# A decoder block on one core: the weights of group B's projections, of group A's queries and of the cross keys are split without GpSimd

## The chip, the core and the metric

The kernel runs on one core of a Trainium2 chip. A core has TensorE (matrix products and transposes), VectorE, ScalarE and GpSimd (elementwise work), SyncE (which here only issues transfers) and 16 DMA engines. The time is that of one execution on the device, in microseconds; the median of the runs shown is 813.85.

## The reference

The kernel computes one decoder layer for 512 tokens of width 1024 in float32, and a final RMSNorm:

```
h = rmsnorm(x);  proj = h @ w_in                       # one projection, 2984 columns
# group A (8 heads): indexer -> top-k keys per query -> attention over latents
index = sum_h relu(q_idx . k_idx) * w_idx;  sel = top_k(causal index, 128)
q_lat = q_nope @ w_uk;  s = q_lat . c_kv + q_rope . k_rope;  o_A = softmax(s[sel]) @ c_kv @ w_uv
# group B (8 heads): causal windows (128,1), (512,4), (2048,16), merged by softmax denominators
o_B = merge(dilated_attention(rope(q), rope(k), v))
x = x + concat(o_A, o_B) @ w_out
x = x + cross_attention(rmsnorm(x), rmsnorm(mem))      # 4 heads, 256 memory tokens
x = x + square(relu(rmsnorm(x) @ w_up)) @ w_down
out = rmsnorm(x)
```

## The kernel before

Every weight matrix is taken as the sum of a high and a low part, and a product as three TensorE products (`mm3`: high by high, high by low, low by high). So a weight passes four steps before TensorE can use it: SyncE's queue loads a piece of 128x1024 (or 128x768) into `wraw`; a cast makes the high part `whi` (line 130 on ScalarE, or line 128 on VectorE); a subtraction makes the low part `wlo` = `wraw` - `whi` (line 131, on GpSimd or VectorE); then TensorE reads both. `wraw` has three buffers, `whi` and `wlo` six each. `split_unit` does one piece; its letter says where: "v" casts on ScalarE and subtracts on VectorE, "p" casts on ScalarE and subtracts on GpSimd, "V" and "P" are the same with the cast on VectorE. `load_weight` splits a matrix into pieces and takes the letters in turn.

The stages, in the order in which they are written: norm and transposes of x; the indexer's projections and scores (lines 365 to 378: products and additions into `ghi` and `glo` on VectorE); group B's values, queries and keys (from line 381); for the four blocks of 128 queries, group B's attention (`attend`), interleaved with group A's queries (`queries_a`, two halves of four heads), the top-k rounds (`top_k`, lines 557 and 558: MAX8 and MATCH_REPLACE8 on VectorE, 16 rounds per block) and the norm of the memory tokens; group A's keys and attention; the cross keys (`keys_cross`, two halves of four pieces); output projection, cross-attention, MLP.

In `attend` a group of heads goes through a chain: scores on TensorE into one of two PSUM banks `sc`; line 426 on VectorE adds the bias and takes the extreme, which frees the bank; the exponential on ScalarE (line 428); reciprocal and scaling on VectorE (lines 429, 431); transposes on TensorE (`tp`, line 113), copies, and the product with the values (`pv`).

The order of the instructions on each engine is set by a scheduler when the program is built: it simulates a time line and places every instruction where its inputs and a free engine let it. So a change of an instruction's engine also changes the order of others. In the running program each engine takes its own list strictly in order.

Of the kernel before, what the change touches and what calls it, by code (L numbers as in the profile page):

```python
# [38 lines left out]
C_QN, C_QR, C_CKV, C_KR, C_QI, C_KI, C_WI, C_QB, C_KB, C_VB = (  # L39
    0, 512, 768, 896, 928, 1440, 1504, 1512, 2024, 2536)  # L40
# [24 lines left out]
def kernel(  # L65
# [16 lines left out]
    def nm(s):  # L82
        uid[0] += 1
        return f"{s}_{uid[0]}"

    def mtile(shape, dt, tag, bufs=1, pool=None):
        return (pool or main).tile(shape, dt, name=nm(tag), tag=tag, bufs=bufs)
# [7 lines left out]
    def bank_mm():  # L95
        return bank("mm", 3)

    def bank_tp():
        return bank("tp", 2)
# [12 lines left out]
    def tpose(*a, **k):  # L112
        ins = nc.tensor.transpose(*a, **k)  # L113
        if ordered[0]:
            tc.keep_in_program_order(ins)
# [8 lines left out]
    def split_unit(raw, hi, lo, how="v"):  # L124


        if how in "PV":
            nc.vector.tensor_copy(hi, raw)  # L128
        else:
            nc.scalar.copy(hi, raw)  # L130
        (nc.gpsimd if how in "pP" else nc.vector).tensor_tensor(lo, raw, f32(hi), op=ALU.subtract)  # L131

    def load_weight(w, segs, k0, how, between=None):


        n = sum(c1 - c0 for c0, c1 in segs)
        nk = 4 if n <= 256 else 2
        his, los = [], []
        for u in range(KD // nk):
            raw = mtile([P, nk, n], F32, "wraw", 3)  # L140
            hi = mtile([P, nk, n], F32R, "whi", 6)
            lo = mtile([P, nk, n], F32R, "wlo", 6)
            rows = w[(k0 + nk * u) * P:(k0 + nk * u + nk) * P, :].rearrange("(k p) c -> p k c", p=P)
            o = 0
            for c0, c1 in segs:
                nc.sync.dma_start(raw[:, :, o:o + c1 - c0], rows[:, :, c0:c1])
                o += c1 - c0
            split_unit(raw, hi, lo, how[u % 4])
            if between is not None:
                between(u)  # L150
            for j in range(nk):
                his.append(hi[:, j, :])
                los.append(lo[:, j, :])
        return his, los
# [17 lines left out]
    def mm3(dst, a, b, first=True, last=True, ks=None, again=False):  # L172


        n = len(a[0])
        for k in ks if ks is not None else range(n):
            mmul(dst, a[0][k], b[0][k], start=first and k == 0, stop=False, skip_group_check=again)
            mmul(dst, a[0][k], b[1][k], start=False, stop=False, skip_group_check=again)
            mmul(dst, a[1][k], b[0][k], start=False, stop=last and k == n - 1, skip_group_check=again)
# [36 lines left out]
    def split_from(ps, hi, lo):  # L216
        nc.scalar.copy(hi, ps)
        nc.vector.tensor_tensor(lo, ps, f32(hi), op=ALU.subtract)
# [23 lines left out]
    w_in0 = w_in[0]  # L242
# [27 lines left out]
    def h_tok(t):  # L270
        return ([hT[0][:, k, t * P:(t + 1) * P] for k in range(KD)],
                [hT[1][:, k, t * P:(t + 1) * P] for k in range(KD)])

    def rope(ps, heads, half, tabs, t, dst, dup=None):


        cos, sin, nsin = (tab[:, t, None, :].to_broadcast([P, heads, half]) for tab in tabs)
        r = r_mix[:, t:t + 1]
        n = heads * 2 * half
        rb = tmp.tile([P, 512], F32, name=nm("rb"), tag="rb", bufs=2)  # L280
        rbv = rb[:, :n].rearrange("p (h c f) -> p h c f", h=heads, c=2)
        if dup is None:
            ra = dst
        else:
            ra = tmp.tile([P, 512], F32, name=nm("ra"), tag="tok", bufs=2)[:, :n].rearrange(
                "p (h c f) -> p h c f", h=heads, c=2)

        def times(o, i, tab):
            nc.vector.scalar_tensor_tensor(o, i, r, tab, op0=ALU.mult, op1=ALU.mult)  # L289

        for c in range(2):
            times(ra[:, :, c, :], ps[:, :, c, :], cos)
        times(rbv[:, :, 0, :], ps[:, :, 1, :], nsin)
        times(rbv[:, :, 1, :], ps[:, :, 0, :], sin)
        if dup is None:
            nc.vector.tensor_tensor(*(a.rearrange("p h c f -> p h (c f)") for a in (dst, ra, rbv)), op=ALU.add)  # L296
        else:
            for c in range(dup):
                nc.vector.tensor_tensor(dst[:, :, c, :], ra.rearrange("p h c f -> p h (c f)"),
                                        rbv.rearrange("p h c f -> p h (c f)"), op=ALU.add)  # L300
# [78 lines left out]


    vB = [mtile([P, 2, 512], F32, f"u3{c}") for c in "ab"]
    wv = load_weight(w_in0, [(C_VB, C_VB + 512)], 0, "vpvp")
    for t in range(NT):
        ps = bank_mm()
        mm3(ps, h_tok(t), wv)
# [1 line left out]
    qkB = []  # L387
    for tag, col in (("u2a", C_QB), ("u2b", C_KB)):
        dst = mtile([P, 4, S], F32, tag)
        wt = load_weight(w_in0, [(col, col + 512)], 0, "pppp")  # L390
        for t in range(NT):
            ps = bank_mm()
            mm3(ps, h_tok(t), wt)
            tok = tmp.tile([P, 512], F32, name=nm("tok"), tag="tok", bufs=2)
            rope(ps.rearrange("p (h c f) -> p h c f", h=NH, c=2), NH, 32, tab64, t,
                 tok.rearrange("p (h c f) -> p h c f", h=NH, c=2))
            tp = bank_tp().rearrange("p (j t) -> p j t", j=4)
            for j in range(4):
                tpose(tp[:, j, :], tok[:, j * P:(j + 1) * P], ident)
            nc.scalar.copy(dst[:, :, t * P:(t + 1) * P], tp)  # L400
        qkB.append(dst)
# [70 lines left out]

    qA = mtile([96, NH, S], F32, "u1")
    def queries_a(g):
        wt = load_weight(w_in0, [(C_QN + 256 * g, C_QN + 256 * g + 256), (C_QR + 128 * g, C_QR + 128 * g + 128)], 0, "pppp")
        for t in range(NT):
            ps = bank_mm()
            mm3(ps[:, :384], h_tok(t), wt)
            tok = tmp.tile([P, 512], F32, name=nm("tok"), tag="tok", bufs=2)
            tokv = tok[:, :384].rearrange("p (h f) -> p h f", h=4)  # L480
            nc.scalar.activation(tokv[:, :, 0:64], ps[:, 0:256].rearrange("p (h f) -> p h f", h=4), AF.Copy,
                                 scale=r_mix[:, t:t + 1])
            rope(ps[:, 256:384].rearrange("p (h c f) -> p h c f", h=4, c=2), 4, 16, tab32, t,
                 tokv[:, :, 64:96].rearrange("p h (c f) -> p h c f", c=2))
            tp = bank_tp().rearrange("p (j t) -> p j t", j=4)
            for j in range(4):
                tpose(tp[0:96, j, :], tokv[:, j, :], ident)
            nc.scalar.copy(qA[:, 4 * g:4 * g + 4, t * P:(t + 1) * P], tp[0:96])
# [79 lines left out]
    def keys_cross(i):  # L568
        memT = state["memT"]
        if i == 0:  # L570
            state["kc"] = [mtile([P, KD, MEM], F32R, f"u2{c}") for c in "ab"]
        kc = state["kc"]
        wt = load_weight(w_kv[0], [(512 * i, 512 * i + 512)], 0, "pppp")
        for m in range(4):
            ps = bank_mm()
            msl = slice(m * P, (m + 1) * P)
            mm3(ps[:, :MEM], ([a[:, msl] for a in wt[0]], [a[:, msl] for a in wt[1]]),
                ([memT[:, 0, k, :] for k in range(KD)], [memT[:, 1, k, :] for k in range(KD)]))
            split_from(ps[:, :MEM], kc[0][:, 4 * i + m, :], kc[1][:, 4 * i + m, :])


    group_b(0)
    queries_a(0)
    top_k(1)
    group_b(1)
    top_k(2)
    queries_a(1)
    memory()
    group_b(2)
# [5 lines left out]
    for i in range(2):  # L595
        keys_cross(i)
# [109 lines left out]
    for i in range(2):  # L706
        wt = load_weight(w_q[0], [(512 * i, 512 * i + 512)], 0, "PPPP")
# [58 lines left out]
    for i in range(2):  # L766
        wt = load_weight(w_kv[0], [(D + 512 * i, D + 512 * i + 512)], 0, "ppPP")
# [75 lines left out]
    for g in range(4):  # L843
# [6 lines left out]
        for i in range(2):  # L850
            c0 = 1024 * g + 512 * i
            wt = load_weight(w_up[0], [(c0, c0 + 512)], 0, "vvvv")
# [143 lines left out]
```

## Time and profile before

| what | value |
|---|---|
| median of 3 runs | 813.85 us (813.5 to 816.56) |
| profiled execution | 814.07 us, its span 812.3 us |
| TensorE busy | 785.9 us (97%) |
| VectorE busy | 560.0 us (69%) |
| ScalarE busy | 382.5 us (47%) |
| GpSimd busy | 215.4 us (27%) |
| subtractions of line 131 on `wraw`, GpSimd | 59, together 139.3 us |
| the same on VectorE | 64, together 80.6 us |

A profile shows one execution. An engine's busy time is the sum of its instructions, and the span runs from the first to the last. A timeline row gives an instruction's start, its length, engine, line, what it writes and reads with the shape, how many alike follow at once, and in brackets how long the engine stood idle before it and what it waited for. The windows give each engine's busy time in a stretch, then TensorE's mean granted clock as a share of full speed.

### The profile page before, as it was taken

The numbers are of one execution on the slowest core, as the hardware profiler recorded it, in microseconds if no ns is written. First come the engines' busy times: TensorE is split into PE (matmuls) and PEld (weight loads), VectorE is DVE, ScalarE is ACT, GpSimd is POOL, SyncE is SP. The second block draws the span as 40 slices with busy tenths as digits, with TensorE's granted clock in tenths as the row PEclk, the third lists the DMA queues.
The fourth block names the chain that finished last, engine by engine and source line by source line (L and its number), as shares of the span: only waits on it lengthen the run. The fifth ranks groups of instructions, "written<-read, shape, count | busy, mean of one in ns | idle before, by whom it ended". The sixth has DMA issues, their size and how long they took to land.

```text
span 812.3 us, 11144 instructions
## 1 busy us (share of the span) xinstructions
PE 785.9 (97%) x4066; PEld 649.0 (80%) x4066; DVE 560.0 (69%) x1169; ACT 382.5 (47%) x743; POOL 215.4 (27%) x164
## 2 busy tenths in 40 slices
PE   6799999999999999999999999999999999999995
PEld 5688878985698778788898888888888888888884
DVE  6775999998668844634683447767776776676674
ACT  5444333457955634222472545533552455345544
POOL 4733143130613406544510201110111011201132
PEclk9899999999999999999999999999999999999998
DMA  8441232202423303322540333496439743963482
GB/s 288 133 119 38 69 105 73 66 1 78 156 79 105 105 1 103 102 80 79 181 140 18 103 104 82 101 229 212 99 83 209 225 100 85 223 221 85 89 164 103
DMA packets 53223, 94.12 MB, mean 116 GB/s; under 512 B 5265, under 2 KB 11057, under 8 KB 53169
## 3 DMA queue, kind: packets, MB, share of 16 engines
q1 hardware_dynamic: 44464, 76.64, 30.1%
q0 software_dynamic: 8704, 16.78, 12.4%
q8 instruction: 32, 0.52, 0.3%
q14 instruction: 23, 0.18, 0.1%
HBM read 90.78 MB, written 2.10 MB: 114 GB/s over the span
## 4 chain that ended last, share of the span: by engine, by line
PE 82%; DVE 10%; issue 3%; POOL 2%; ACT 2%; DMA 1%; SPq 0%; POOLq 0%; ACTq 0%; DVEq 0%
PE mm L107 61%; PE sc L107 11%; PE tp L113 5%; PE pv L107 3%; PE tp L107 2%; DVE glo L558 1%; DVE m L557 1%; DVE ghi L377 1%; ACT whi L130 1%; DMA u2b<-in_w_down_dram 1%; DVE whi L128 1%; DVE rb L289 1%; DVE kk L296 0%; DMA u2a<-in_x_dram 0%; DVE wlo L131 0%
## 5 line engine op out<-in xcount | busy, mean ns | idle before, releaser
L131 POOL TENSOR_TENSOR wlo<-wraw,whi 128x1024 fp32r<-128x1024 f32 (+2 forms) x59 | 139.3, 2379 | 186.8 <-ACT whi L130 156.7
L107 PE MATMUL mm<-whi,h 128*128 128x512 f32 (+2 forms) x536 | 165.3, 377 | 6.9 <-DVE h L231 3.5
L130 ACT CAST whi<-wraw 128x1024 fp32r<-128x1024 f32 (+3 forms) x111 | 114.0, 1029 | 93.9 <-PE mm L107 42.4
L107 PE MATMUL mm<-h,whi 128*128 128x512 f32 (+1 forms) x448 | 153.2, 366 | 0.0
L107 PE MATMUL mm<-u,whi 128*128 128x512 f32 x320 | 125.0, 390 | 0.0
L107 PE MATMUL mm<-u,wlo 128*128 128x512 f32 x320 | 124.7, 390 | 0.0
L107 PEld LDWEIGHTS mm<-whi,h 128*128 128x128 f32 x536 | 100.6, 194 | 21.6 <-DVE h L231 3.9
L107 PE MATMUL mm<-wlo,h 128*128 128x512 f32 (+2 forms) x280 | 104.9, 376 | 0.1
L131 DVE TENSOR_TENSOR wlo<-wraw,whi 128x1024 fp32r<-128x1024 f32 (+1 forms) x64 | 80.6, 1260 | 29.7 <-ACT whi L130 29.4
L107 PEld LDWEIGHTS mm<-h,whi 128*128 128x128 f32 x448 | 80.7, 188 | 14.7 <-issue 1.2
L895 POOL DMA_DIRECT2D u2b<-in_w_down_dram x24 | 32.6, 1369 | 224.5 <-DMA wraw<-in_w_down_dram 120.6
L107 PE MATMUL mm<-whi,ghi 128*128 128x512 f32 x192 | 76.2, 397 | 0.0
L107 PE MATMUL mm<-wlo,ghi 128*128 128x512 f32 x192 | 75.7, 394 | 0.0
L107 PE MATMUL mm<-whi,glo 128*128 128x512 f32 x192 | 75.1, 391 | 0.0
L107 PEld LDWEIGHTS mm<-u,wlo 128*128 128x128 f32 x320 | 60.1, 188 | 12.5
L107 PEld LDWEIGHTS mm<-u,whi 128*128 128x128 f32 x320 | 60.1, 188 | 12.2
L131 DVE TENSOR_TENSOR wlo<-u2b,whi 128x1024 fp32r<-128x1024 f32 x32 | 39.1, 1225 | 30.2 <-ACT whi L130 30.2
L107 PEld LDWEIGHTS mm<-wlo,h 128*128 128x128 f32 x280 | 54.1, 194 | 7.2 <-DVE wlo L131 0.5
L130 ACT CAST whi<-u2b 128x1024 fp32r<-128x1024 f32 x32 | 33.6, 1052 | 48.0 <-DMA u2b<-in_w_down_dram 39.5
L428 ACT ACTIVATE p<-p,mx 128x128 f32<-128x128 f32 (+3 forms) x64 | 35.9, 563 | 26.4 <-DVE mx L426 26.3
L862 ACT ACTIVATE sq<-r 128x512 f32<-128x512 f32 x32 | 20.2, 631 | 49.1 <-DVE r L860 49.1
L860 DVE SCALAR_TENSOR_TENSOR r<-mm,rT 128x512 f32<-128x512 f32 x32 | 22.0, 688 | 30.3 <-PE mm L107 23.2
(250 smaller groups left out, 1433.7 us busy)
## 6 DMA issues: line engine op xcount, KB each, us to landing
wraw<-in_w_up_dram SPq DMA_DIRECT2D x32, 512.0 KB, 4.7
wraw<-in_w_down_dram SPq DMA_DIRECT2D x24, 512.0 KB, 6.1
u2b<-in_w_down_dram POOLq DMA_DIRECT2D x24, 512.0 KB, 7.6
wraw<-in_w_in_dram SPq DMA_DIRECT2D x16, 512.0 KB, 4.0
wraw<-in_w_kv_cross_dram SPq DMA_DIRECT2D x16, 512.0 KB, 3.7
wraw<-in_w_out_dram SPq DMA_DIRECT2D x8, 512.0 KB, 3.8
wraw<-in_w_q_cross_dram SPq DMA_DIRECT2D x8, 512.0 KB, 3.7
wraw<-in_w_o_cross_dram SPq DMA_DIRECT2D x8, 512.0 KB, 3.7
```

The costliest lines, as they stand in the source:

```text
L107: ins = nc.tensor.matmul(*a, **k)
L113: ins = nc.tensor.transpose(*a, **k)
L128: nc.vector.tensor_copy(hi, raw)
L130: nc.scalar.copy(hi, raw)
L131: (nc.gpsimd if how in "pP" else nc.vector).tensor_tensor(lo, raw, f32(hi), op=ALU.subtract)
L289: nc.vector.scalar_tensor_tensor(o, i, r, tab, op0=ALU.mult, op1=ALU.mult)
L377: nc.vector.scalar_tensor_tensor(acc[b], rl[:, :n], wh, acc[b], op0=ALU.mult, op1=ALU.add)
L428: nc.scalar.activation(pr[:, c], pr[:, c], AF.Exp, bias=mx[:, i:i + 1], scale=-1.0, accum_out=sm[:, i:i + 1])
L557: nc.vector.max(m8, acc[b])
L860: nc.vector.scalar_tensor_tensor(r, ps, 0.0, rows_ready[0], op0=ALU.max, op1=ALU.mult)
L862: nc.scalar.activation(sq, r, AF.Square)
L895: nc.gpsimd.dma_start(xw[:, u], src, accum_op=ALU.add)
```

## The change

Four calls of `load_weight` get other letters, so that 26 subtractions run on VectorE instead of GpSimd: 2 of group B's values (line 382), 8 of its queries and keys (line 390), 8 of 128x768 of group A's queries (line 475) and 8 of the cross keys (line 573). The casts stay on ScalarE, and other weights keep their letters.

```diff
     vB = [mtile([P, 2, 512], F32, f"u3{c}") for c in "ab"]
-    wv = load_weight(w_in0, [(C_VB, C_VB + 512)], 0, "vpvp")
+    wv = load_weight(w_in0, [(C_VB, C_VB + 512)], 0, "vvvv")
...
         dst = mtile([P, 4, S], F32, tag)
-        wt = load_weight(w_in0, [(col, col + 512)], 0, "pppp")
+        wt = load_weight(w_in0, [(col, col + 512)], 0, "vvvv")
...
     def queries_a(g):
-        wt = load_weight(w_in0, [(C_QN + 256 * g, C_QN + 256 * g + 256), (C_QR + 128 * g, C_QR + 128 * g + 128)], 0, "pppp")
+        wt = load_weight(w_in0, [(C_QN + 256 * g, C_QN + 256 * g + 256), (C_QR + 128 * g, C_QR + 128 * g + 128)], 0, "vvvv")
...
         kc = state["kc"]
-        wt = load_weight(w_kv[0], [(512 * i, 512 * i + 512)], 0, "pppp")
+        wt = load_weight(w_kv[0], [(512 * i, 512 * i + 512)], 0, "vvvv")
```

The first place is VectorE at the end of the indexer's block 1 (`glo_110`) and the start of block 2 (`ghi_109`). Before, from the product that ends at 72.48:

```order
L377 SCALAR_TENSOR_TENSOR glo_110_645<-rl_685,weff,glo_110_645 128x256
L377 SCALAR_TENSOR_TENSOR glo_110_645<-rl_691,weff,glo_110_645 128x256
L378 TENSOR_TENSOR glo_110_645<-glo_110_645,bias 128x128
L557 MAX m_297_1555<-glo_110_645 128x8
L558 MATCH_REPLACE glo_110_645<-m_297_1555,glo_110_645 128x256
L375 TENSOR_SCALAR ghi_109_644<-rl_698,weff 128x384
```

The same place after the change; wlo_938 and wlo_944 are pieces of group B's queries, wlo_1103 and wlo_1109 of its keys:

```order
L377 SCALAR_TENSOR_TENSOR glo_110_645<-rl_685,weff,glo_110_645 128x256
L131 TENSOR_TENSOR wlo_938<-wraw_936,whi_937 128x1024
L377 SCALAR_TENSOR_TENSOR glo_110_645<-rl_691,weff,glo_110_645 128x256
L131 TENSOR_TENSOR wlo_944<-wraw_942,whi_943 128x1024
L378 TENSOR_TENSOR glo_110_645<-glo_110_645,bias 128x128
L131 TENSOR_TENSOR wlo_1103<-wraw_1101,whi_1102 128x1024
L557 MAX m_297_1555<-glo_110_645 128x8
L375 TENSOR_SCALAR ghi_109_644<-rl_698,weff 128x384
L558 MATCH_REPLACE glo_110_645<-m_297_1555,glo_110_645 128x256
L131 TENSOR_TENSOR wlo_1109<-wraw_1107,whi_1108 128x1024
```

Four subtractions now stand between the indexer's instructions, which wait behind them and behind their casts.

The second place is VectorE in group B's attention of the last block (p_2303 to p_2362 are its softmax tiles, in the order of the heads). Before:

```order
L431 TENSOR_SCALAR p_2303<-p_2303,rc_2306 128x512
L429 RECIPROCAL rc_2323<-sm_2322 128x1
L431 TENSOR_SCALAR p_2320<-p_2320,rc_2323 128x512
L426 ISA p_2345,mx_2346<-sc_2343,bias 128x512
L426 ISA mx_2346 128x1
L429 RECIPROCAL rc_2348<-sm_2347 128x1
L431 TENSOR_SCALAR p_2345<-p_2345,rc_2348 128x512
```

After; wlo_3047 and wlo_3053 are pieces of the cross keys, wlo_2194 (a few rows ahead) the split of group A's key weights, sel_2298 the end of the last top-k:

```order
L558 MATCH_REPLACE ghi_109_644<-m_493_2295,ghi_109_644 128x512
L426 ISA p_2362,mx_2363<-sc_2360,bias 128x512
L426 ISA mx_2363 128x1
L131 TENSOR_TENSOR wlo_3047<-wraw_3045,whi_3046 128x1024
L429 RECIPROCAL rc_2323<-sm_2322 128x1
L218 TENSOR_TENSOR glo_266_1364<-pv_2021,ghi_265_1363 128x2x128
L560 TENSOR_SCALAR sel_2298<-ghi_109_644 128x512
L429 RECIPROCAL rc_2348<-sm_2347 128x1
L131 TENSOR_TENSOR wlo_3053<-wraw_3051,whi_3052 128x1024
L431 TENSOR_SCALAR p_2320<-p_2320,rc_2323 128x512
L429 RECIPROCAL rc_2365<-sm_2364 128x1
L431 TENSOR_SCALAR p_2345<-p_2345,rc_2348 128x512
```

Two subtractions of the cross keys, the last top-k round and another head's score step have come between the softmax steps of p_2320 and p_2345.

The third place is TensorE at the same heads (mm_2203 to mm_2230 are group A's keys). Before:

```order
L107 MATMUL mm_2215<-cT_238,wlo_2194 128x512
L113 MATMUL tp_2328<-ident,p_2320 128x128 x4
L107 MATMUL sc_2402<-u2b_1100,u2a_923 128x512
L113 MATMUL tp_2353<-ident,p_2345 128x128 x4
L107 MATMUL sc_2427<-u2b_1100,u2a_923 128x512
L107 MATMUL sc_2444<-u2b_1100,u2a_923 128x512
L107 MATMUL mm_2221<-cT_238,whi_2193 128x512
```

After:

```order
L107 MATMUL mm_2215<-cT_238,wlo_2194 128x512
L107 MATMUL sc_2402<-u2b_1100,u2a_923 128x512
L113 MATMUL tp_2328<-ident,p_2320 128x128 x4
L113 MATMUL tp_2353<-ident,p_2345 128x128 x4
L107 MATMUL mm_2221<-cT_238,whi_2193 128x512
L107 MATMUL mm_2221<-cT_239,whi_2193 128x512
L107 MATMUL mm_2221<-cT_238,wlo_2194 128x512
```

The scores of sc_2402 have moved ahead of the transposes of p_2320, and those of sc_2427 to a place behind nine products of group A's keys, the transposes of p_2362 and a product with the values.

## Rows read from the trace of the kernel before

**Rows 1.** Busy time of each engine; the chain that ended last, by engine

```profile
PE 785.9 (97%) x4066; PEld 649.0 (80%) x4066; DVE 560.0 (69%) x1169; ACT 382.5 (47%) x743; POOL 215.4 (27%) x164
...
PE 82%; DVE 10%; issue 3%; POOL 2%; ACT 2%; DMA 1%; SPq 0%; POOLq 0%; ACTq 0%; DVEq 0%
```

**Rows 2.** Windows: columns in the first row, one stretch in each other

```profile
core 0: us, PE busy (x) PEld busy (x) DVE busy (x) ACT busy (x) POOL busy (x), PEclk, DMA share, GB/s
44.00:72.48 28.48, 28.48 (x139) 23.46 (x139) 16.34 (x32) 12.74 (x25) 7.57 (x3) 1.00 0.27 74
...
182.00:204.60 22.60, 21.46 (x137) 12.24 (x135) 17.85 (x68) 17.32 (x53) 0.00 (x0) 1.00 0.29 81
72.48:204.60 132.12, 129.48 (x731) 104.22 (x730) 123.21 (x369) 65.54 (x154) 38.11 (x20) 1.00 0.23 66
204.60:222.00 17.40, 16.52 (x93) 11.40 (x93) 12.00 (x27) 16.16 (x31) 12.64 (x6) 0.90 0.52 167
222.00:295.00 73.00, 72.14 (x567) 58.85 (x565) 52.77 (x160) 38.35 (x103) 21.41 (x9) 1.00 0.25 80
```

**Rows 3.** Timeline of VectorE, 70 to 82 (start, length, ...)

```profile
71.99 0.48 DVE L377 SCALAR_TENSOR_TENSOR glo<-rl,weff,glo 128x256 f32<-128x256 f32 x1 [1.36 <-ACT rl L372]
75.01 2.44 DVE L377 SCALAR_TENSOR_TENSOR glo<-rl,weff,glo 128x256 f32<-128x256 f32 x1 [2.53 <-ACT rl L372]
77.48 2.38 DVE L378 TENSOR_TENSOR glo<-glo,bias 128x128 f32<-128x128 f32 x1
...
80.76 1.58 DVE L375 TENSOR_SCALAR ghi<-rl,weff 128x384 f32<-128x384 f32 x1
```

**Rows 4.** Timeline of VectorE, 100 to 111

```profile
100.68 0.27 DVE L378 TENSOR_TENSOR ghi<-ghi,bias 128x128 f32<-128x128 f32 x1
...
101.73 1.93 DVE L375 TENSOR_SCALAR ghi<-rl,weff 128x512 f32<-128x512 f32 x1
...
106.87 1.93 DVE L377 SCALAR_TENSOR_TENSOR ghi<-rl,weff,ghi 128x512 f32<-128x512 f32 x1
...
110.44 0.73 DVE L377 SCALAR_TENSOR_TENSOR ghi<-rl,weff,ghi 128x512 f32<-128x512 f32 x1
```

**Rows 5.** Timeline of GpSimd, the four subtractions at 74.77

```profile
74.77 9.83 POOL L131 TENSOR_TENSOR wlo<-wraw,whi 128x1024 fp32r<-128x1024 f32 x4 [16.41 <-ACT whi L130]
```

**Rows 6.** Timeline of VectorE, a subtraction at 34.47 and its successor

```profile
34.47 1.22 DVE L131 TENSOR_TENSOR wlo<-wraw,whi 128x1024 fp32r<-128x1024 f32 x1
35.60 0.35 DVE L296 TENSOR_TENSOR kk<-kk,rb 128x64 f32<-128x64 f32 x2
```

**Rows 7.** Timeline of VectorE, 204 to 212

```profile
204.11 0.49 DVE L431 TENSOR_SCALAR p<-p,rc 128x512 f32<-128x512 f32 x1
204.51 0.68 DVE L218 TENSOR_TENSOR wlo<-tp,whi 128x512 fp32r<-128x512 f32 x1
205.11 0.68 DVE L426 CUSTOM_DVE_ANT_0 p<-sc,bias 128x512 f32<-128x512 f32 x1
...
206.55 0.42 DVE L218 TENSOR_TENSOR glo<-pv,ghi 128x256 fp32r<-128x256 f32 x1 [0.75 <-ACT ghi L217]
...
208.89 1.49 DVE L431 TENSOR_SCALAR p<-p,rc 128x512 f32<-128x512 f32 x1
...
211.02 1.30 DVE L544 COPY h<-mm 64x512 f32<-64x512 f32 x2
```

**Rows 8.** Timeline of TensorE, 115.34 and 206 to 212

```profile
115.34 0.63 PE L113 MATMUL tp<-ident,tok 128*128 128x128 f32 x4 [0.95 <-DVE tok L296]
...
206.87 0.60 PE L113 MATMUL tp<-ident,p 128*128 128x128 f32 x4
207.40 1.12 PE L107 MATMUL sc<-u2b,u2a 64*128 64x512 f32 x2
...
211.04 1.23 PE L107 MATMUL sc<-u2b,u2a 64*128 64x512 f32 x2 [0.88 <-DVE mx L426]
```

**Rows 9.** Timeline of ScalarE, a cast at 80.86

```profile
80.86 1.05 ACT L130 CAST whi<-wraw 128x1024 fp32r<-128x1024 f32 x1 [0.54 <-DMA wraw<-in_w_in_dram]
```

## The prediction

> **What bounds the kernel now.** I read the page first: TensorE is busy for 785.9 of 812.3 us, VectorE for 560.0, and the chain that ended last is TensorE for 82% and VectorE for 10% [rows 1]. The reader is to see an engine that hardly ever rests, so an edit on other engines changes the time only through the moments in which TensorE waits for them, or newly has to.
>
> Next I read the busy time by stretch [rows 2], because an average over the span hides where VectorE is full. Between 72.48 and 204.60 us, where the indexer, the top-k rounds and group B's attention lie, TensorE is busy for 129.48 of 132.12 us and VectorE for 123.21. Its 8.91 us of rest are mostly at the end: 4.75 in 182 to 204.6, so 4.16 before that. Before this stretch (44 to 72.48) VectorE rests 12.1 of 28.5 us, after it (222 to 295) 20.2 of 73. Thus work added to VectorE is free on either side and not in the middle.
>
> Third, I read VectorE's instructions in order of time. A product-and-add of line 377 takes 0.48 us, but 2.44 at 75.01; the mask addition of line 378 takes 0.27 at its normal size, but 2.38 at 77.48 [rows 3, 4]. Both lie inside GpSimd's four subtractions that run from 74.77 for 9.83 us [rows 5]. A VectorE instruction with two operands in the on-chip memory, or a 128x384 scaling, is held until GpSimd's subtraction ends. So GpSimd's help is not free: it costs VectorE some us.
>
> Last, TensorE's own waits in the middle are few: 0.95 us at 115.34 for a rotated query tile, 0.88 at 211.04 for a score bank, and a stretch at 204.6 to 222 with a mean granted clock of 0.90, part of it at the lower of the two levels, 1.2 instead of 2.4 GHz, after the rest at 211.04 [rows 2, 8].
>
> **The change part by part.** It moves 26 subtractions (line 131) from GpSimd to VectorE: 2 for group B's values, 8 for its queries and keys, 8 of 128x768 for group A's queries, 8 for the cross keys. The casts stay on ScalarE, the loads on SP's queue in the same order; GpSimd's list of instructions loses 26 rows.
>
> *Price of one.* A subtraction of 128x1024 on VectorE lasts 1.22 us, and the next instruction starts 1.13 us after it [rows 6]; I use 1.13. For 128x768 there is no row. It lies between the spacing of a 128x512 subtraction (line 218 at 204.51, the next start at 205.11: 0.60) and 1.13 [rows 6, 7]; I take the middle, 0.87. On GpSimd one took about 2.4 us (9.83 / 4) [rows 5], off everyone's path but for the blocking.
>
> *First four* (both of the values, two of the queries; 4 x 1.13 = 4.5 us). They fall before 72.48, in 12.1 us of rest: nothing.
>
> *The middle.* From the seventh line-377 product (ends 72.48) to the scaling of p_2345 (starts 204.11, ends 204.60) VectorE now also has nine subtractions of 128x1024 (two of the queries, four of the keys, three of the cross keys, which the new order puts ahead of group B's last softmaxes): 9 x 1.13 = 10.2. Eight of 128x768 for group A's queries: 8 x 0.87 = 7.0 (4.8 to 9.0 by the bounds). Some rows that stood behind p_2345 now stand ahead of it: a line-218 subtraction of 128x512 (0.68), a score step (0.68) and a line-218 subtraction of 128x256 (0.42), less the overlap of about 0.1 each, with a reciprocal of 0.16: 1.7 [rows 7]. Sum 18.9.
>
> *What goes.* Blocked instructions return to their normal size: 2.44 - 0.48 = 1.96, 2.38 - 0.27 = 2.11, the 128x384 scaling 1.58 - 0.49 = 1.09 (0.49 is the 128x512 one, so at least this), and the 128x512 ones at 106.87 and 101.73, 1.93 - 0.73 = 1.20 and 1.93 - 0.49 = 1.44 [rows 3, 4, 7]. Sum 7.8 in the middle. The blocked scaling at 208.89 (1.49 for 0.49) lies behind p_2345 and gives 1.0 back there, which is within what I take for hand-offs below.
>
> *VectorE's new time.* Busy 123.2 + 18.9 - 7.8 = 134.3. I keep the 4.16 of rest before 182, which is made of waits for casts and scores; the 4.75 behind it is filled, since the new order pulls top-k rounds of the last block apart into it. p_2345 is then scaled at 72.48 + 134.3 + 4.2 = 211.0, 6.4 later than at 204.60; p_2320, one reciprocal and one scaling before it, at about 210.3.
>
> *What TensorE feels.* It transposes p_2320 at 206.87 [rows 8], so it waits 210.3 - 206.9 = 3.4. In the new order the scores of sc_2402 (1.12) go ahead of this transpose: -1.1. The scores of sc_2427 wait for a bank that VectorE clears three copies of line 544 (about 0.65 each), a scaling (0.49), wlo_3059 (1.13), a 128x256 subtraction (0.42) and a score step (0.68) later [rows 7], 4.6 us behind 211.0, so at about 215.6; TensorE has some 4.5 us of other work behind 210.3 (an estimate from the spacing of its rows, [rows 8]) and is there at 214.8: +0.8. The wait of 0.88 at 211.04 has another neighbour and goes: -0.9. Small hand-offs, and a clock that falls after a rest as it does in 204.6 to 222 (17.4 x 0.10 = 1.7 us there [rows 2]), lie between 0 and 4; I take 1.7, the one such row. Sum 3.4 - 1.1 + 0.8 - 0.9 + 1.7 = +3.9.
>
> *The last four* (cross keys, 4 x 1.13 = 4.5; the fifth is wlo_3059 above). They lie in 204.6 to 222 with 5.4 us of rest and 222 to 295 with 20.2 [rows 2]: nothing, and TensorE reads their results microseconds after. If that cover is gone, each costs at most its 1.1.
>
> *The added wait.* A VectorE subtraction waits for its cast, and the cast for its load; at 80.86 ScalarE's cast had to wait 0.54 for the load [rows 9]. VectorE works in order, so what is behind such a subtraction (softmax steps, line 377) waits as well. In the new order wlo_3053 stands directly ahead of p_2320's scaling. Lower bound 0, upper some 4 us (a subtraction's whole 2.4 on GpSimd and the load's wait); I take 0 for the forecast and keep the rest for a rival.
>
> The profiled execution took 814.07 us for a span of 812.3, and the median of the runs is 813.85. So 814.07 + 3.9 = 818.0, or **817.8** on the median's scale.
>
> *A rule weighed.* The blocked rows [rows 3 to 5] say that GpSimd's help costs VectorE 7.8 us here. The Trainium skill, page "SBUF — State Buffer", section "SBUF: two separate sides", says that VectorE and GpSimd share one port pair as an exclusive lock, and that the loser blocks for the whole instruction; the trace agrees (2.44 for 0.48). By that alone VectorE would be early by 7.8 and the kernel faster, which is rival A. Against it stands the page "Perfetto Trace Analysis", section "Optimizing Scalar/DVE Operations": a saturated VectorE may hand work even to GpSimd, though with the shared port this may not help. The rows decide between the two: 17.2 us of subtractions come in, 7.8 go out.
>
> **Rivals.** *A, the locks decide.* VectorE's added work is in the top-k filler, which nobody awaits, and what TensorE awaits comes earlier, since nothing is held any more. Then the waits of 0.95 and 0.88 go, and the slow stretch of 1.7: 813.85 - 3.5 = 810.3, and some tenths of smaller waits less, about **810**. For it: the blocked instructions are real, and the new order was free to place the subtractions. Against it: VectorE's sum is positive by 9.4 without the pulled rows, and only 4.75 us of rest are there to take it.
>
> *B, slower than forecast.* The mechanism is VectorE's order: a subtraction whose cast is late holds the softmax steps behind it between 184 and 222, once ahead of p_2320 and once at the bank of sc_2427. Two waits of some 2 us (a load's wait of 0.54 and a cast of 1.05 each [rows 9], and a hand-off) come on top: 817.8 + 4 = **822**. It decides from the point where a cross-key cast ends later than VectorE reaches its subtraction. For it: ScalarE is busy 16.16 of 17.4 us in 204.6 to 222. Against it: VectorE itself is late there, so that casts have more time.
>
> *C, no change.* The forecast's lateness is 3.4 us at one place. If the 128x768 price is at its lower end (7.0 to 4.8: -2.2) and the rows pulled ahead of p_2345 come at moments of rest after all (-1.7), the 3.4 are gone, and what is left of the sum (0.8 - 0.9 and some hand-offs) makes 813.85 + 1 = **815**.
>
> **How the numbers follow.** A change of 0.5% is 4.1 us, about what a measurement here can tell: faster is below 809.8, slower above 817.9. Chances: forecast 0.40 with 815 to 821 as its own range, A 0.14, C 0.25, B 0.21. Slower is B and half of the forecast, 0.41; faster is most of A with its tail below 809.8, 0.13; the rest 0.46. The range goes from A's edge, 810, to 824, beyond B, and leaves out about 2 in 10.
>
> **What would show it.** In the profile after, VectorE should be busy for about 9 us more between 72 and 205, line 377's instructions should all be near 0.5 to 0.7, and GpSimd empty there but for the norm of the memory. The step on lateness is right if TensorE waits 2 to 5 us around 207 to 216 for VectorE's scalings or score steps; it is wrong if these waits are under 1 us in all (C), or if the first transposes of group B's queries lose their waits and the stretch ends earlier (A). Waits of VectorE for ScalarE's casts ahead of softmax steps would show B. A load landing late, with SP's queue in another order, would make the whole sum wrong.

## The result, and the profile after

The changed kernel takes 1.0055 times the time of the kernel before, with a 95% interval of 1.0033 to 1.0077; on the median of the kernel before in the same comparison, 815.43 us (21 runs, 813.46 to 818.21), that is 819.9 us. Its own 21 runs have a median of 826.96 us and fall into two groups that the granted clock tells apart, 816.0 to 819.3 us (10 runs, median 816.8, mean clock 0.990 to 0.994) and 827.0 to 835.6 us (11 runs, 0.963 to 0.976); the ratio leaves out the 8 slowest runs of the second group, so half of the executions are slower than it says. The profile after shows a run of the second group (829.65 us, span 827.9); experiment 1 gave a profile of the first (816.43 us, span 814.7).

The page of the profile after, TensorE's line of busy times and the granted clock in 40 slices:

```profile
PE 799.6 (97%) x4066; PEld 655.3 (79%) x4066; DVE 572.1 (69%) x1195; ACT 383.4 (46%) x743; POOL 156.1 (19%) x138
...
PEclk9899999995799999999999999999999999999998
```

GpSimd's work fell from 215.4 to 156.1 us, and VectorE's rose from 560.0 to 572.1 [rows 1]. TensorE is busy for 13.7 us more with the same 4066 products. The clock is down to 5 and 7 tenths in slices 10 and 11 (186 to 228 us). The windows around them, in the profile after (columns as in [rows 2]):

```profile
core 0: us, PE busy (x) PEld busy (x) DVE busy (x) ACT busy (x) POOL busy (x), PEclk, DMA share, GB/s
180.00:187.00 7.00, 5.67 (x28) 3.18 (x26) 6.90 (x25) 5.39 (x16) 0.00 (x0) 0.91 0.62 159
187.00:215.00 28.00, 26.75 (x88) 13.73 (x88) 18.00 (x59) 11.10 (x32) 0.00 (x0) 0.50 0.05 17
215.00:222.00 7.00, 7.00 (x33) 3.88 (x32) 6.34 (x15) 6.51 (x13) 0.00 (x0) 0.90 0.45 153
```

The same windows in the profile without the fall:

```profile
180.00:187.00 7.00, 5.67 (x27) 2.73 (x25) 6.99 (x26) 5.50 (x17) 0.00 (x0) 1.00 0.72 188
187.00:215.00 28.00, 25.05 (x139) 13.99 (x140) 27.94 (x81) 22.53 (x53) 0.00 (x0) 1.00 0.27 85
215.00:222.00 7.00, 7.00 (x52) 4.63 (x52) 5.68 (x15) 5.30 (x11) 0.00 (x0) 1.00 0.53 152
```

In 180 to 187 both have TensorE busy for 5.67 of 7 us. Then the one runs 28 us at 0.50 (1.2 GHz), which is 14 us of work lost, and the other at 1.00. The first meets two more waits of 0.62 us in that stretch:

```profile
192.58 1.12 PE L107 MATMUL pv<-pT,u3a 128*64 128x128 f32 x8 [0.62 <-ACT pT L441]
...
202.19 1.12 PE L107 MATMUL pv<-pT,u3a 128*64 128x128 f32 x8 [0.62 <-ACT pT L441]
```

The spans differ by 827.9 - 814.7 = 13.2. So what the change does is read from the second profile, and what the fall costs from the difference.

VectorE in the second profile, the instructions that answer to [rows 3, 4] and one of the moved 128x768 subtractions:

```profile
75.46 0.48 DVE L377 SCALAR_TENSOR_TENSOR glo<-rl,weff,glo 128x256 f32<-128x256 f32 x1
...
77.08 0.28 DVE L378 TENSOR_TENSOR glo<-glo,bias 128x128 f32<-128x128 f32 x1
...
78.76 0.40 DVE L375 TENSOR_SCALAR ghi<-rl,weff 128x384 f32<-128x384 f32 x1
...
104.61 0.95 DVE L131 TENSOR_TENSOR wlo<-wraw,whi 128x768 fp32r<-128x768 f32 x1
```

None of these is blocked: 0.48 for 2.44, 0.28 for 2.38, 0.40 for 1.58. The smaller subtraction lasts 0.95, and the next instruction starts 0.87 behind it (at 105.48). VectorE's windows in the same profile:

```profile
72.43:182.00 109.57, 109.42 (x613) 93.77 (x611) 102.87 (x300) 49.32 (x107) 7.32 (x6) 1.00 0.23 64
182.00:204.60 22.60, 19.68 (x115) 10.45 (x116) 22.60 (x80) 16.31 (x44) 0.00 (x0) 1.00 0.26 70
73.86:210.88 137.02, 133.17 (x737) 105.47 (x737) 131.27 (x391) 71.02 (x163) 7.32 (x6) 1.00 0.26 73
```

Between 182 and 204.6 it has no rest at all (22.60 of 22.60; before, 17.85 [rows 2]). TensorE's listed waits from 182 us to 222, where the kernel before has 0.88 at 211.04 [rows 8] and three smaller ones (0.33, 0.49, 0.29; 1.99 in all):

```profile
182.35 0.41 PE L113 MATMUL mm<-ident,ghi 128*128 128x128 f32 x2 [0.50 <-DVE rb L289]
183.58 0.91 PE L107 MATMUL sc<-u2b,u2a 64*128 64x384 f32 x2 [0.82 <-DVE mx L426]
...
189.56 0.66 PE L107 MATMUL pv<-pT,u3a 128*64 128x128 f32 x8 [0.62 <-ACT pT L441]
...
195.22 0.66 PE L107 MATMUL pv<-pT,u3a 128*64 128x128 f32 x8 [0.62 <-ACT pT L441]
...
202.12 0.66 PE L113 MATMUL tp<-ident,wraw 128*128 128x128 f32 x4 [0.30 <-ACT pT L441]
...
210.57 1.08 PE L113 MATMUL tp<-ident,p 128*128 128x128 f32 x8 [0.78 <-DVE rc L429]
...
214.86 0.66 PE L107 MATMUL pv<-pT,u3a 128*64 128x128 f32 x8 [0.42 <-DVE glo L218]
```

They add up to 4.06 us, while from 72 to 182 TensorE now rests only 109.57 - 109.42 = 0.15 us (1.5 before [rows 2]).

TensorE's own work has changed as well. Score products of two heads that follow each other directly run side by side, so that four take the time of two; in the new order none of the 512-wide ones do. Two rows, the first from the kernel before, the second from the second profile:

```profile
197.76 1.13 PE L107 MATMUL sc<-u2b,u2a 64*128 64x512 f32 x4
...
196.51 1.12 PE L107 MATMUL sc<-u2b,u2a 64*128 64x512 f32 x2
```

Group B's scores of all four widths keep TensorE busy for 19.1 us in the kernel before and for 20.9 in the second profile. So between these two profiles TensorE rests 1.4 us less up to 182 and 2.1 more from there to 222, works 1.8 longer on scores, and is spared the 1.7 of the lower clock at 204.6 to 222: +0.8 together. The spans differ by 2.4 (814.7 and 812.3) and the medians by 1.3 (816.8 and 815.4); the remainder is not resolved.

### The profile page after: what moved, and what is told of

Read it like the earlier page. It is cut to its first block, busy times and chain, and to the rows that moved or that the text cites. A ratio compares the mean times of both kernels' runs of the same rounds, so it can differ in the third digit from the quotient of the medians.

```text
span 827.9 us, 11151 instructions
## 1 busy us (share of the span) xinstructions
PE 799.6 (97%) x4066; PEld 655.3 (79%) x4066; DVE 572.1 (69%) x1195; ACT 383.4 (46%) x743; POOL 156.1 (19%) x138
## 4 chain that ended last, share of the span: by engine, by line
PE 86%; DVE 6%; issue 3%; POOL 2%; ACT 2%; DMA 1%; POOLq 0%; ACTq 0%
PE mm L107 63%; PE sc L107 13%; PE tp L113 5%; PE pv L107 3%; PE tp L107 2%; DVE wlo L131 1%; DMA u2b<-in_w_down_dram 1%; ACT whi L130 1%; DVE whi L128 1%; DVE kk L296 0%; PE mm L113 0%; DVE glo L218 0%; DMA u2a<-in_x_dram 0%; DVE xr L920 0%; DVE nmx L734 0%
## 5 line engine op out<-in xcount | busy, mean ns | idle before, releaser
L131 DVE TENSOR_TENSOR wlo<-wraw,whi 128x1024 fp32r<-128x1024 f32 (+2 forms) x90 | 110.4, 1227 | 32.6 <-ACT whi L130 32.1
L131 POOL TENSOR_TENSOR wlo<-wraw,whi 128x1024 fp32r<-128x1024 f32 (+1 forms) x33 | 79.0, 2404 | 138.8 <-PE mm L107 77.5
L107 PEld LDWEIGHTS mm<-whi,glo 128*128 128x128 f32 x192 | 36.0, 188 | 8.3 <-issue 0.7
L107 PEld LDWEIGHTS mm<-whi,ghi 128*128 128x128 f32 x192 | 36.1, 188 | 7.4 <-issue 0.5
```

Source lines behind the costliest of these rows:

```text
L107: ins = nc.tensor.matmul(*a, **k)
```

## The experiments

Ratios are to the kernel before on the same chip, with 95% intervals. Theory 1 is the prediction's: VectorE's load pushes its work late, and TensorE waits for it; here it was joined by the clock that falls behind such waits.

**1. The changed kernel again** (no edit).

> The changed kernel once more, beside the parts below. Theory 1 (VectorE's load): up to 182 us TensorE is some 2 us ahead of the kernel before, since VectorE is no longer held; then the last block's top-k rounds, pushed late by the added subtractions, stand ahead of softmax steps, and TensorE waits twice at 183 to 185 (0.5 and 0.8 us in the trace after). Where the granted clock then falls to 0.5 for some 28 us the time is 827 to 830, where it does not, 816 to 819. Rival 2 (the clock falls by itself, whatever the kernel does): the same stretch falls in the parts as well, and in the kernel before. Rival 3 (late casts of the cross keys hold softmax steps): VectorE waits for ScalarE's casts between 196 and 222.

Ratio 1.0062 (1.0023 to 1.0100); 6 of 12 runs at 815.8 to 816.8 us, 6 at 826.8 to 833.6, near the two ranges that theory 1 gave. Of the 114 runs of the kernel before in all comparisons here none was over 822.04, so a fall of this length belongs to the changed kernel: against rival 2. What VectorE does at the two waits:

```profile
182.38 0.68 DVE L557 MAX8 m<-ghi 128x8 f32<-128x512 f32 x1
182.98 0.54 DVE L426 CUSTOM_DVE_ANT_0 p<-sc,bias 128x384 f32<-128x384 f32 x1
...
208.82 1.21 DVE L131 TENSOR_TENSOR wlo<-wraw,whi 128x1024 fp32r<-128x1024 f32 x1
209.94 0.48 DVE L431 TENSOR_SCALAR p<-p,rc 128x512 f32<-128x512 f32 x1
...
210.41 0.47 DVE L431 TENSOR_SCALAR p<-p,rc 128x512 f32<-128x512 f32 x1
```

At 182.38 a top-k MAX8 stands between the rotation and the score step of 182.98, and TensorE, which needs the bank, waits till 183.58. At 208.82 wlo_3053 stands ahead of p_2320's scaling, and p_2345 is scaled at 210.41. None of these rows has an idle time for a cast, and between 184 and 222 only one subtraction waited for one (0.73, at 221.5, behind the softmax steps in question): against rival 3.

**2. Group B's projections alone.**

```diff
-    wv = load_weight(w_in0, [(C_VB, C_VB + 512)], 0, "vpvp")
+    wv = load_weight(w_in0, [(C_VB, C_VB + 512)], 0, "vvvv")
-        wt = load_weight(w_in0, [(col, col + 512)], 0, "pppp")
+        wt = load_weight(w_in0, [(col, col + 512)], 0, "vvvv")
```

> Only group B's projections are split without GpSimd (10 subtractions). Theory 1: the instructions blocked at 75 to 112 return to normal (7.8 us of VectorE back for 6.8 us of subtractions in the middle), TensorE's waits at 106 and 115 go, and about 4 top-k rounds (5 us) fall behind the first softmax of block 2; TensorE is 2 us ahead at 182 and loses about 1 of it later: 811 to 814. Rival 2: no different from the kernel before in its stretch at half clock. Rival 3: the whole gain stays, 810 to 812, as no cross key is touched.

Missed by all three: 1.0076 (1.0051 to 1.0101), all 6 runs at 817.8 to 824.2. TensorE's waits, and the windows behind the first and the last of them:

```profile
182.97 0.41 PE L113 MATMUL mm<-ident,ghi 128*128 128x128 f32 x2 [0.47 <-DVE rb L289]
184.46 0.91 PE L107 MATMUL sc<-u2b,u2a 64*128 64x384 f32 x2 [1.08 <-DVE mx L426]
...
192.03 1.12 PE L107 MATMUL pv<-pT,u3a 128*64 128x128 f32 x8 [0.62 <-ACT pT L441]
...
215.09 1.12 PE L107 MATMUL sc<-u2b,u2a 64*128 64x512 f32 x2 [1.35 <-DVE mx L426]
```

```profile
184.00:200.00 16.00, 14.91 (x53) 8.59 (x54) 11.83 (x46) 9.64 (x29) 0.00 (x0) 0.58 0.28 84
212.00:228.00 16.00, 14.65 (x76) 9.40 (x76) 11.55 (x25) 11.77 (x24) 9.49 (x4) 0.79 0.51 166
```

A pair of waits, 0.47 and 1.08, is followed by a mean clock of 0.58, and 1.35 at 215.09 by one of 0.79. This part alone makes the kernel slower. The wait of 1.35 is not VectorE's load: the cross keys are still subtracted on GpSimd here, and the scaling ahead of that score step lasts 2.45 us instead of 0.49.

```profile
211.98 2.45 DVE L431 TENSOR_SCALAR p<-p,rc 128x512 f32<-128x512 f32 x1
```

**3. Group A's queries alone.**

```diff
-(w_in0, [(C_QN + 256 * g, C_QN + 256 * g + 256), (C_QR + 128 * g, C_QR + 128 * g + 128)], 0, "pppp")
+(w_in0, [(C_QN + 256 * g, C_QN + 256 * g + 256), (C_QR + 128 * g, C_QR + 128 * g + 128)], 0, "vvvv")
```

> Only group A's queries are split without GpSimd (8 subtractions of 128x768, 7 us by 0.87 each). Theory 1: VectorE gets 7 us more and keeps its blocked instructions at 75 to 112, so the last top-k ends some 7 us later, in the softmax steps of blocks 2 and 3; TensorE waits at 183 to 187 for 1 to 3 us, and the clock may fall: 815 to 819, or 826 to 830 where it falls. Rival 3: no change, 813 to 815, since no cross key is touched.

1.0007 (0.9994 to 1.0021), median 815.4: no difference, which is rival 3's figure and the lowest end of theory 1's. The added 7 us push VectorE's work late here too (0.91 below, 0.33 before), and the clock falls for a short while behind the pair (0.87 in 187 to 200), but the wait of 0.95 at 115 [rows 8] is gone:

```profile
184.31 0.41 PE L113 MATMUL mm<-ident,ghi 128*128 128x128 f32 x2 [0.91 <-DVE rb L289]
...
186.09 0.91 PE L107 MATMUL sc<-u2b,u2a 64*128 64x384 f32 x2 [0.49 <-DVE mx L426]
...
210.56 2.06 PE L107 MATMUL sc<-u2b,u2a 64*128 64x512 f32 x4 [0.73 <-DVE mx L426]
```

**4. The cross keys alone.**

```diff
-        wt = load_weight(w_kv[0], [(512 * i, 512 * i + 512)], 0, "pppp")
+        wt = load_weight(w_kv[0], [(512 * i, 512 * i + 512)], 0, "vvvv")
```

> Only the cross keys are split without GpSimd (8 subtractions, 9 us). The order up to the first softmax of block 2 is that of the kernel before. Theory 1: VectorE has rest from 182 us on (4.75 us up to 204.6, and more later), so 813 to 815. Rival 3: the subtractions hold softmax steps behind late casts, TensorE waits 2 us or more between 200 and 222, 816 to 820.

0.9990 (0.9975 to 1.0006). As theory 1 had it, median 814.7; rival 3's 816 to 820 is refuted.

**5 and 6. Less of VectorE's other work**, in the kernel before and in the changed one.

```diff
-        for i in range(TOPK // 8):
+        for i in range(TOPK // 8 - (4 if b == 3 else 0)):
```

> The kernel before, with 4 of the 16 top-k rounds of the last block of queries left out (about 5 us of VectorE's work; the choice of keys in that block is then not the reference's). Theory 1 (VectorE's load in 72 to 205 us decides): in the kernel before the last round ends before the first softmax of block 2, so there is little to gain: the waits of 0.33 and 0.49 at 185 and 0.88 at 211 may go with the half-clock stretch behind the last, 811 to 814.5. Rival 2 (the time comes from something else than VectorE's load): no change, within 1 us of the kernel before.

> The changed kernel with the same 4 top-k rounds left out. Theory 1: the 5 us that the change adds to VectorE are taken out again, while its instructions stay unblocked: the waits at 183 and between 189 and 215 shrink below 1 us each and mostly go, the clock stays at its upper level, and TensorE keeps the 2.6 us that it has gained by 150 us: 809 to 812, in every execution, without those of 827 to 830. Rival 2 (not VectorE's load but the new order, or the clock by itself): 815 to 817, with executions of 827 to 830 among them as before.

Before: 0.9988 (0.9970 to 1.0005), no gain clear of noise; the median of 814.1 fits theory 1 and, nearly, rival 2. Changed: 0.9980 (0.9962 to 0.9997), with 7 of 12 runs at 812.0 to 813.7, and 5 at 825.4 to 832.9. So taking out the same 5 us of VectorE's work brought 1.1 us in the kernel before, within the noise, and some 3.2 us after (medians of the runs without the fall, 816.1 in experiment 1 and 812.9 here; 3.6 if each is taken against the kernel before on its chip), as theory 1 says. But theory 1's 809 to 812 was missed, as was rival 2's 815 to 817, and the second group stayed, against what I had expected. In its profile the first waits are as they were:

```profile
182.50 0.41 PE L113 MATMUL mm<-ident,ghi 128*128 128x128 f32 x2 [0.51 <-DVE rb L289]
183.73 1.08 PE L107 MATMUL sc<-u2b,u2a 64*128 64x384 f32 x2 [0.82 <-DVE mx L426]
...
192.54 1.12 PE L107 MATMUL pv<-pT,u3a 128*64 128x128 f32 x8 [0.62 <-ACT pT L441]
```

The rounds taken away are the last ones. Those that stand between the instructions at 182 us remained.

**7 and 8. Neither engine**: the subtraction left out, the high part taken for the low one, in every piece of the matrices named. That takes in the two pieces of group B's values that the kernel before already subtracts on VectorE: 12 subtractions in experiment 7, 28 in experiment 8.

```diff
     def split_unit(raw, hi, lo, how="v"):
+        if how == "n":
+            return nc.scalar.copy(hi, raw)
...
-            lo = mtile([P, nk, n], F32R, "wlo", 6)
+            lo = hi if how[u % 4] == "n" else mtile([P, nk, n], F32R, "wlo", 6)
```

> The kernel before without the 10 subtractions of group B's projections on either engine: TensorE takes the high part in place of the low part, so the products are less exact but as many. Neither lock nor added load. Theory 1: as group B's part of the change up to 150 us (2 to 3 us ahead), and nothing is given back: 810 to 812. Rival 2 (locks cost nothing, the change's loss is the order alone): within 1 us of the kernel before.

> The kernel before without all 26 subtractions, the high part taken in place of the low one in the same way. This is the floor of what moving them could bring. Theory 1: TensorE's waits of 0.33, 0.95, 0.33, 0.49, 0.29 and 0.88 and the half-clock stretch of 1.7 go for the most part: 809.5 to 811.5. Rival 2: 813 to 815.

Group B's: 0.9934 (0.9910 to 0.9958), median 808.6. All: 0.9909 (0.9888 to 0.9930), median 807.25, no run over 808.0. Both are below what I had expected. In the first TensorE has two listed waits left between 60 and 222 us, in the second none:

```profile
204.75 1.12 PE L107 MATMUL sc<-u2b,u2a 64*128 64x512 f32 x2 [0.77 <-DVE mx L426]
...
211.11 0.50 PE L107 MATMUL mm<-whi,cT 128*128 128x512 f32 x1 [0.42 <-DVE h L544]
```

So these subtractions, 26 of the 28 on GpSimd, cost about 7.4 us in the kernel before (815.23 x 0.0091), and more with the 26 on VectorE. Rival 2 falls.

**9. The changed kernel without the rounds at 182 us.**

```diff
-        for i in range(TOPK // 8):
+        for i in range(TOPK // 8 - (8 if b == 3 else 0)):
```

> The changed kernel with the last 8 of the 16 top-k rounds of the last block left out, so that the order has no round any more between the instructions of 180 to 186 us (leaving out only 4 left those rounds in place, and the waits of 0.5 and 0.8 at 183 with them). If these two waits, close together, are what makes the clock fall to 0.5, then they shrink to those of the kernel before (0.3 and 0.5) or less, no execution takes 825 or more, and the time is 809 to 812. If the clock falls for another reason (the new order elsewhere, or by itself), 4 to 6 of 12 executions still take 825 to 833.

0.9908 (0.9879 to 0.9938), all 5 runs at 807.9 to 808.6, 1 us below the expectation. VectorE goes from the rotation to the score step with one instruction of line 231 between, and TensorE's only listed wait in 60 to 222 us is that of the second fence. The eight rounds are also some 10 us less of VectorE's work, and another order, so this run alone does not tell the rounds' place from their load:

```profile
180.72 0.46 DVE L289 SCALAR_TENSOR_TENSOR rb<-mm,r_mix,tabs 128x64 f32<-128x64 f32 x2
181.11 0.34 DVE L231 SCALAR_TENSOR_TENSOR h<-mm,gT,h 128x128 fp32r<-128x128 f32 x1
181.48 0.56 DVE L426 CUSTOM_DVE_ANT_0 p<-sc,bias 128x384 f32<-128x384 f32 x1
```

```profile
182.10 0.91 PE L107 MATMUL sc<-u2b,u2a 64*128 64x384 f32 x2 [0.28 <-DVE mx L426]
```

**10 to 12. Parts of the change that might be faster**: the first halves of group B's queries and keys, the second halves, and the second halves with the cross keys.

```diff
-        wt = load_weight(w_in0, [(col, col + 512)], 0, "pppp")
+        wt = load_weight(w_in0, [(col, col + 512)], 0, "vvpp")   # 10
+        wt = load_weight(w_in0, [(col, col + 512)], 0, "ppvv")   # 11, 12
...
+        wt = load_weight(w_kv[0], [(512 * i, 512 * i + 512)], 0, "vvvv")   # 12
```

> Of group B's queries and keys only the first two pieces each are subtracted on VectorE, 4 of the 26; all else as in the kernel before. Two of the four fall in VectorE's rest before 72 us. Theory 1 (blocking against load): VectorE gets 2.3 us in its full stretch and loses some of its 7.8 us of blocking, and the last top-k round ends just ahead of the first softmax of block 2 in the new order, so that no round stands between the softmax steps: 811 to 814. Rival (any subtraction moved there costs its 1.1 us): 815 to 818.

> Of group B's queries and keys only the last two pieces each are subtracted on VectorE, also 4 of the 26. All four fall in VectorE's full stretch (4.5 us), and the last top-k round falls two instructions behind the first softmax of block 2. Theory 1: as the first halves or up to 2 us slower, 812 to 816, with waits at 183 to 186 near those of the kernel before. Rival (any subtraction moved costs its 1.1 us): 818 and more.

> The second halves of group B's queries and keys and all cross keys on VectorE, 12 of the 26 subtractions, put together because the first alone was somewhat faster than the kernel before and the second no slower. Theory 1 (VectorE has rest behind 182 us, so the cross keys cost nothing there, and their blocking at 205 to 222 goes): 809 to 813, at or up to 1 us below the second halves alone. Rival 3 (the cross keys' subtractions hold softmax steps between 204 and 222, now that the last top-k round ends later): 813 to 817.

First halves 1.0012 (0.9987 to 1.0037), runs 812.8 to 821.5; second halves 0.9967 (0.9939 to 0.9995), runs 810.2 to 819.6; with the cross keys 0.9959 (0.9939 to 0.9980), median 811.25. The times of the second and third are as expected; the first, expected at 811 to 814 and found at 816.3, fits its rival, and the order of the first two is the reverse of my forecast (their intervals just overlap). The profile of the first halves has the pair of 0.4 and 0.8 again; in that of the last version the pair is 1.22 and 0.49, where I had expected, for the second halves, waits near those of the kernel before, and the wait at 210 is no longer listed:

```profile
183.71 0.41 PE L113 MATMUL mm<-ident,ghi 128*128 128x128 f32 x2 [0.42 <-DVE rb L289]
184.94 0.91 PE L107 MATMUL sc<-u2b,u2a 64*128 64x384 f32 x2 [0.82 <-DVE mx L426]
...
209.86 1.12 PE L107 MATMUL sc<-u2b,u2a 64*128 64x512 f32 x2 [0.87 <-DVE mx L426]
```

```profile
183.99 0.41 PE L113 MATMUL mm<-ident,ghi 128*128 128x128 f32 x2 [1.22 <-DVE rb L289]
184.89 1.72 PE L107 MATMUL sc<-u2b,u2a 64*128 64x384 f32 x4 [0.49 <-DVE mx L426]
```

The last version beats the kernel before by 0.4%, and by their ratios the changed one by about 1%. Its profile is of one of its slower runs (814.92), in which the clock fell behind the pair:

```profile
187.00:200.00 13.00, 12.92 (x64) 8.07 (x64) 8.39 (x34) 8.50 (x26) 0.00 (x0) 0.61 0.16 51
```

A mean of 0.61 over 13 us is some 10 us at the lower level, 5 us of work, against 28 and 14 in the profile after. No wait is listed in these 13 us, and two of 0.62 in those 28; experiment 2, with one (at 192.03), has 13 us (0.50 in 187 to 200). That the later waits make the fall last is not tested. Why the second pair lets the clock fall less often (a mean clock of 0.988 or less in 3 and 2 of 12 runs, against 6 of 12 with the first halves) is open.

## Why the prediction was right, step by step

*The sum on VectorE* held. The scaling of p_2345 was forecast to end at 211.0 and ended at 210.88 (210.41 + 0.47), that of p_2320 at 210.3 and ended at 210.42. That it came so close is in part luck, as the parts were split otherwise: the seventh line-377 product ended at 73.86, not 72.48, VectorE was busy from there for 131.27 us, not 134.3, and rested for 137.02 - 131.27 = 5.75, not 4.2. The price of 0.87 for a 128x768 subtraction was right.

*Where the lateness is felt* was wrong. I compared the new time with TensorE's old place, 206.87, and got one wait of 3.4 less 1.1. In fact only 0.78 was left at p_2320 (210.57), and 0.42 at 214.86; the prediction's sign, 2 to 5 us around 207 to 216, did not come. TensorE had met five waits of 2.86 us from 182 us on. Two of them, 1.32, are for VectorE, because the top-k rounds that I had treated as filler stand in one list with the rotations and softmax steps. Three, 1.54, are for ScalarE's copies: in the new order the transposes stand directly ahead of the product that reads their copy. Experiment 9 takes eight rounds away, which changes the order too, and of the five one of 0.28 is left. The sign of about 9 us more for VectorE between 72 and 205 failed as well: in 72.43 to 204.6 it is busy for 102.87 + 22.60 = 125.5 us, 2.3 more than before, since it could not be more than full.

*TensorE's own work* was taken as fixed, a term put at nothing without a reason. Score products that stand apart cost 1.8 us more in the changed kernel.

*The blocking* was real and undersized. Rival A's 3.5 us came from listed waits and the clock. Without the subtractions on any engine it is 5.4 us for group B's (experiment 7) and 7.4 us for all. TensorE's rest in [rows 2], 2.64 and 0.88 us, and the 1.7 of the clock cover 5.2 of the 7.4; group B's scores, more often side by side there (16.6 us for 19.1), cover the rest.

*The clock* was the term that failed in size: 1.7 us, with 4 as the upper bound. In half of the runs it is 13.2 us, when two waits of 0.5 and 0.8 within 2 us are followed by 28 us at 1.2 GHz; 11 of the 21 runs lie beyond the range's 824, for which the sum had no term. That this pair is the cause is supported by experiment 9 (none of 5 runs) against 6 (5 of 12, pair in place), but a run with the same pair keeps its clock as often, so what tips it is not known. Five runs are few, and the kernel before with eight rounds less was not tried.

*Rivals.* B's mechanism (late casts ahead of softmax steps) did not occur at the steps in question. C's time was near for the first group of runs: 816.8, the median of its ten, is within 0.5% of the kernel before, but C's reason, that nothing is late, is refuted by the waits from 182 us on. A's half was true up to 182 us, and its gain was given back afterwards. The forecast of 817.8 lies between the 816.8 of that group and the 819.9 of the ratio. Its 3.9 us were put together from waits at other places than the measured ones, without TensorE's own work and with a smaller clock, so the number is in part luck.

## What to carry to other kernels

Work that moves to an engine that is full in one stage is paid there, but not at the place where the sum is drawn: look for the first instruction behind the added work that another engine awaits, filler or not. Compare the order on the bottleneck too: an engine's busy time for the same instructions changed here with what stood next to what. Moving a part can be better than moving all: here 12 of 26, found by trial, were better than all and than none. Two short waits of TensorE close together were followed, in half of the runs, by a loss of ten times their length, so compare many runs, not one profile.

## What the runs showed of the hardware

The same program, with TensorE busy for 5.67 of 7 us at the same place in two profiles, went on at 1.00 in the one and at 0.50 for 28 us in the other; by time and mean clock, it stayed up in 16 of 33 runs and fell in 17. The pair of 0.33 and 0.49 us in the kernel before was not seen to lead to it in its profile (the clock there is 1.00 in 182 to 204.6 [rows 2]). The 4 us that I had taken as the most that hand-offs and clock could cost are less than a third of the 13.2. Four 64-row score products took 1.13 us when two heads followed each other, and two took 1.12 when they did not.
